# A two-layer encoder on one core: gate and up start together, one fewer output-projection unit, three split buffers, shorter bias and softmax

## The chip, the core and the metric

The kernel runs on one core of a Trainium2 chip. The metric is the device time of one execution in microseconds. The engines are named as in the profile: PE (TensorE matmuls), PEld (its weight loads), ACT (ScalarE), DVE (VectorE), POOL (GpSimd) and SP (SyncE, which issues most DMAs).

## The reference

The inputs are 256 positions of width 1024, in fp32; there are two layers, each an attention sublayer and a feed-forward sublayer, each with a residual.

```python
def mixer_sublayer(x, ...):
    h = rms_norm(x, n1)
    qa, ka, va, qd, kd, vd, qc, kc, vc = split(h @ w_in_l)
    qa, ka = rms_norm(qa, qg[0]), rms_norm(ka, kg[0])
    out_a = neighbourhood_attention(qa, ka, va, rpb_l, ...)      # 4 heads, bias from rpb
    qd, kd = partial_rotary(rms_norm(...)), ...
    out_d = dilated_window_attention(qd, kd, vd, ...)            # 6 heads
    qc, kc = axial_rotary(rms_norm(...)), ...
    out_c = gqa_block_attention(qc, kc, vc)                      # 6 heads, 2 of keys and values
    mix = concatenate([rms_norm(out_a, ..), rms_norm(out_d, ..), rms_norm(out_c, ..)])
    return x + mix @ w_out_l

def channel_sublayer(x, n2, w_gu, cw, cb, w_dn):
    g, u = split(rms_norm(x, n2) @ w_gu)                         # 2 x 2816 wide
    g = depthwise_conv_centred(g, cw, cb)                        # 3 positions
    return x + (gelu(g) * u) @ w_dn
```

Scores are scaled by 1/8. The neighbourhood heads add a relative bias `rpb` and see only keys within a window.

## The kernel before

**Numbers.** Each fp32 product is made of three matmuls on a high and a low part of both factors (`mm3`, L586; in the feed-forward two, with both parts of the input side by side in a 512 wide moving operand). Activations are split when they are turned (`split_T`, L599: PE transposes 128x128 blocks of `const_x` into `psw`, ACT writes the high part, DVE the low part, into `act_hT`). A weight **unit** has at most 2048 columns on 128 partitions: SP loads it into a `wp_raw` buffer (`load`, L538), then in pieces ACT casts it to `wp_hi` and DVE subtracts into `wp_lo` (`split`, L560). `unit` (L575) hands out the next one, and records the load and the split of later ones: `RAWS, PARTS, AHEAD` (L42) are the raw buffers, the split pairs, and how many units the splits run ahead.

**Order of the work.** `Plan` (L217) records every operation. `order` (L289) then schedules them as a list: at each step it takes, of the operations whose inputs, buffers and engine are ready first by a cost model of its own, the one of lowest rank; the rank is the place in the program plus what `later` adds (`SPLIT_LATER`, `TURN_LATER`, `MIX_LATER`, `PREP_LATER`, L53 on). `emit` (L388) issues them in that order; it fixes each engine's queue, SP's too. All instructions so have one line in the profile, L393, and are told apart by the names of their tiles.

**A layer.** The input is normalised and turned, both halves (L732). `projections` (L737) makes, in `psa` banks, dq, dk, dv, cq, ckv, aqk and av, each of one or two units. Beside them the heads run, in pairs: dilated (`d`), grouped (`c`), neighbourhood (`a`). For each group `prep_d`, `prep_c` and `prep_a` (L1030 to L1061) form `rstd` on POOL (`rstd_of`, L591: `small_ms`, `small_rstd`), scale, and rotate by tables that POOL makes from `const_rot` and the gains (`act_cdq`, `act_sdq`, `act_ccq` and so on, L809, L824). `scores` (L1088) multiplies queries and keys into `psw`, `softens` (L942) takes the maximum (`small_mx`), makes its negative (`small_nm`), and ACT forms the exponentials; `turn` transposes `act_s2k` and splits it into `act_ch` and `act_cl`; `weigh` multiplies with the values; `mixed` (L998) writes `act_mixT_hi`, `act_mixT_lo` and the squares `act_sqm`, which POOL adds. `group_rstd` (L1013) sums the squares with a matmul by `ones` and forms the group's `rstd`; the group's output projections (`out_projections`, L761; tiles po in `psa`) follow, and DVE adds them, scaled, to the residual `const_x`. `OUT_ORDER` has three groups, each in two halves of 512 columns, a unit each; the neighbourhood heads' group comes last.

**The neighbourhood bias.** `na_load` (L692) reads the needed rows of `rpb` into `act_few`; `na_repeat` (L706) scales them on POOL, repeats them 64 times into `act_nab` (28 x 1984) and writes these to a scratch buffer in device memory (`dram_scr`); `na_diagonals` (L716) reads them back along diagonals into `act_nab`, so that each query has its row; `na_bias_mask` (L1076) adds the window's mask in three POOL operations of 128x576. For layer 0 this is recorded beside the first projections, for layer 1 at feed-forward steps 2, 3 and 4 of layer 0 (`NA_STEPS`, L1285); `order` is free to issue the parts sooner.

**From attention to the feed-forward.** Recorded in this order: the first half of the last group's projection, the transposes of half 0 of the new residual, the second half of the projection, the mean square, and then gate step 0 (`half_up(first=True)`, L1196): 16 matmuls on input half 0 (k below 4), the transposes of half 1, 16 matmuls on half 1, and `row_scale`, two transposes that spread the row's `rstd`. Up step 0 follows, 32 matmuls in its own `psw` banks.

**The feed-forward.** 11 steps of 256 columns. `gate` (L1241) joins the high and low sums, multiplies by the row scale, convolves (DVE and ACT) and applies Gelu; `up` (L1260) multiplies with it and splits; `down` (L1270) accumulates into four `psa` banks. The order is G0, U0, G1, D0, U1, G2, D1, U2 and on to G10, U10, D9, D10.

Of the kernel before, what the change touches and what calls it, by code (L numbers as in the profile page):

```python
# [41 lines left out]
RAWS, PARTS, AHEAD, CHUNK = 4, 2, 2, 512  # L42
# [174 lines left out]
class Plan:  # L217
    def __init__(self, tc):
        self.tc, self.ops, self.shift, self.burst, self.bursts = tc, [], 0, None, {}
        for name, short in (("tensor", "PE"), ("scalar", "ACT"), ("vector", "DVE"), ("gpsimd", "POOL"), ("sync", "SP")):  # L220
            setattr(self, name, PlanEngine(self, short, getattr(tc.nc, name)))
# [11 lines left out]
    @contextmanager  # L233
    def together(self):

        self.burst = len(self.bursts)
        self.bursts[self.burst] = []
        yield
        self.burst = None

    def add(self, engine, method, args, kw):
# [39 lines left out]
        for v in outs:  # L281
            v.tile.writes.append((i, v.footprint()))
        o.before.discard(i)
# [152 lines left out]
def encoder_kernel(  # L436
# [84 lines left out]
    def units_of(l):  # L521
# [5 lines left out]
        for gi, c0 in OUT_ORDER:  # L527
            yield rows(w_out[l], *OUTP[gi], c0, 512)
# [6 lines left out]
    views = [v for l in range(DEPTH) for v in units_of(l)]  # L535
    raws, parts, taken = [], [], [0]
# [23 lines left out]
    def split(i):  # L560
# [7 lines left out]
        for c in range(0, n, h):  # L568
# [147 lines left out]
    def na_diagonals(l):  # L716
        scr = nabs["scr"]
        for i in range(2):
# [3 lines left out]
            )  # L722

    load(0)
    for l in range(DEPTH):
# [81 lines left out]


        def tables_d(which, g):  # L809
            cd = act.tile([P, NT, HD], F32, tag=f"cd{which}", name=f"cd{which}{l}", bufs=1)  # L810
            sd = act.tile([P, NT, 16], F32, tag=f"sd{which}", name=f"sd{which}{l}", bufs=1)
            b = lambda v: v.unsqueeze(1).to_broadcast([P, NT, v.shape[1]])
            nc.gpsimd.tensor_tensor(cd, rot[:, :, 0:64], b(g[:, l, 1]), op=ALU.mult)
            for i in range(2):
                o, n = (8 * i, 8 * (1 - i)), 8
                nc.gpsimd.tensor_tensor(
                    sd[:, :, o[0] : o[0] + n],
                    rot[:, :, 64 + o[0] : 64 + o[0] + n],
                    b(g[:, l, 1, o[1] : o[1] + n]),
                    op=ALU.mult,  # L820
                )
            return cd, sd

        def tables_c(which, g):  # L824
            cc = act.tile([P, NT, HD], F32, tag=f"cc{which}", name=f"cc{which}{l}", bufs=1)
            sc = act.tile([P, NT, HD], F32, tag=f"sc{which}", name=f"sc{which}{l}", bufs=1)
            b = lambda v: v.unsqueeze(1).to_broadcast([P, NT, v.shape[1]])
            nc.gpsimd.tensor_tensor(cc, rot[:, :, 80:144], b(g[:, l, 2]), op=ALU.mult)
            for i in range(4):
                o, n = (16 * i, 16 * (i ^ 1)), 16  # L830
                nc.gpsimd.tensor_tensor(
                    sc[:, :, o[0] : o[0] + n],
                    rot[:, :, 144 + o[0] : 144 + o[0] + n],
                    b(g[:, l, 2, o[1] : o[1] + n]),
                    op=ALU.mult,
                )
            return cc, sc
# [99 lines left out]
        class Head:  # L937
# [4 lines left out]
            def softens(self, sps):  # L942
# [4 lines left out]
                mx = small.tile([P, NT], F32, tag="mx", name=f"mx_{name}")  # L947
                rs = small.tile([P, NT], F32, tag="rs", name=f"rs_{name}")
                if bias is not None:
                    sb = act.tile([P, NT, S], F32, tag="s2k", name=f"sb_{name}", bufs=NS2K)  # L950
                    for t in range(NT):
                        nc.vector.tensor_tensor_reduce(
                            sb[:, t], sps[t], bias[t], SCALE, -3e38, ALU.add, ALU.max, mx[:, t : t + 1]
                        )
                    nc.vector.tensor_scalar_mul(nm, mx, -1.0)
                    for t in range(NT):
                        nc.scalar.activation(
                            p[:, t], sb[:, t], AF.Exp, bias=nm[:, t : t + 1], accum_out=rs[:, t : t + 1]
                        )
                else:  # L960
                    for t in range(NT):
                        nc.vector.reduce_max(mx[:, t : t + 1], sps[t], axis=AX.X)
                    nc.vector.tensor_scalar_mul(nm, mx, -SCALE)
                    for t in range(NT):
                        nc.scalar.activation(
                            p[:, t], sps[t], AF.Exp, bias=nm[:, t : t + 1], scale=SCALE,
                            accum_out=rs[:, t : t + 1],
# [62 lines left out]
        def prep_d(which, g):  # L1030
            cd, sd = tables_d(which, g)
# [9 lines left out]
        def prep_c(which, g):  # L1041
            cc, sc = tables_c(which, g)
# [33 lines left out]
        def na_bias_mask():  # L1076
            for i in range(1, NR, 9):
                nv = nabs[l][:, i : i + 9]
                nc.gpsimd.tensor_tensor(
                    nv, nv, na_mask.unsqueeze(1).to_broadcast([P, 9, GRID_W]), op=ALU.add  # L1080
# [115 lines left out]
        def half_up(name, first=False):  # L1196

            wh, wl = unit()
            ps = [psw.tile([P, 2, S], F32, tag="w", name=f"{name}{j}") for j in range(2)]

            def part(j, k):
                js = slice(j * P, (j + 1) * P)
# [3 lines left out]
            if first:  # L1206
                for k in range(4):
                    part(0, k)
                for k in range(4):
                    part(1, k)  # L1210
                split_T(halves(1), h2_hi, h2_lo, 4, gains[:, 2, l, 4:8], f"n2{l}1")
                for k in range(4, KD):
                    part(0, k)
# [163 lines left out]
```

## Time and profile before

| | us |
|---|---|
| median of 3 runs | 625.4 |
| lowest and highest | 625.36, 627.85 |
| the profiled execution, its own time | 626.01 |
| its span in the trace | 624.2 |
| granted clock, mean | 1.00 |
| PE, PEld busy | 608.7, 525.0 |
| DVE, ACT, POOL busy | 490.3, 430.6, 83.3 |
| steady feed-forward, layers 0 and 1 | 148 to 315, 438 to 620 |

The span runs from the first to the last instruction of the trace; the execution's own time is a little longer. Times in the views are from the span's start. A timeline row gives start, duration, engine, line, operation, output and inputs, shapes, and the number of instructions put together in the row; in brackets stands how long the engine was idle before it, and whose end it waited for. Buffer numbers are left out of names.

### The profile page before, as it was taken

How to read it: one execution, taken by the hardware profiler on the slowest of the kernel's cores; microseconds unless marked ns; L12 is line 12 of the kernel's file. 1: busy time of each engine (PE TensorE's matmuls, PEld its weight loads, DVE VectorE, ACT ScalarE, POOL GpSimd, SP SyncE). 2: the span in 40 equal slices, each digit the busy share in tenths (PEclk: the TensorE clock that was granted, in tenths of full speed). 3: DMA queues.
4: the chain of work that ended last, by engine and by line, in shares of the span. 5: the costliest groups of instructions: out<-in, count | busy, mean ns of one | idle time of the engine just before them, and what ended most of it. 6: DMA issues, size and time to landing. Idle time of an engine off the chain costs nothing.

```text
span 624.2 us, 9846 instructions
## 1 busy us (share of the span) xinstructions
PE 608.7 (98%) x3496; PEld 525.0 (84%) x3496; DVE 490.3 (79%) x1026; ACT 430.6 (69%) x1064; POOL 83.3 (13%) x131
## 2 busy tenths in 40 slices
PE   8999999989999999999999999998999999999997
PEld 6998888778888888888899979786888888888885
DVE  4889889798777777777867798978877777877775
ACT  6887998677655655565588799888765655566552
POOL 2764231340000000000023210312000000000000
PEclk9999999999999999999999999999999999999999
DMA  8794312866555555555444632043565655555511
GB/s 279 262 287 154 102 40 96 249 154 213 189 177 178 199 202 202 179 172 173 153 145 154 225 102 85 34 138 136 202 207 199 202 188 170 187 199 188 170 49 67
DMA packets 81345, 104.66 MB, mean 168 GB/s; under 512 B 9464, under 2 KB 68952, under 8 KB 81296
## 3 DMA queue, kind: packets, MB, share of 16 engines
q1 hardware_dynamic: 80720, 103.51, 51.0%
q8 instruction: 27, 0.44, 0.3%
q10 hardware_dynamic: 576, 0.53, 0.3%
q14 instruction: 22, 0.18, 0.1%
HBM read 102.54 MB, written 1.49 MB: 167 GB/s over the span
## 4 chain that ended last, share of the span: by engine, by line
PE 86%; ACT 4%; DVE 4%; DMA 3%; POOL 1%; issue 1%; SPq 0%; ACTq 0%; POOLq 0%; DVEq 0%
PE psw_w L393 47%; PE psa_a L393 39%; ACT act_s2k L393 2%; DMA act_nab<-dram_scr 1%; DVE wp_lo L393 1%; DMA dram_scr<-act_nab 1%; DVE act_s2k L393 1%; POOL small_rstd L393 1%; DVE act_hT L393 1%; DMA act_s2k<-in_norm_g_dram 1%; POOL act_nab L393 0%; ACT L393 0%; ACT wp_hi L393 0%; DVE const_x L393 0%; DVE act_z L393 0%
## 5 line engine op out<-in xcount | busy, mean ns | idle before, releaser
L393 DVE TENSOR_TENSOR wp_lo<-wp_raw,wp_hi 128x512 fp32r<-128x512 f32 (+2 forms) x348 | 248.3, 742 | 50.9 <-ACT wp_hi L393 49.1
L393 PE MATMUL psw_w<-act_hT,wp_hi 128*128 128x512 f32 x704 | 247.4, 396 | 4.7 <-DVE act_hT L393 4.7
L393 ACT CAST wp_hi<-wp_raw 128x512 fp32r<-128x512 f32 (+2 forms) x348 | 213.7, 658 | 25.1 <-PE psw_w L393 15.6
L393 PE MATMUL psw_w<-act_hT,wp_lo 128*128 128x256 f32 x704 | 195.7, 279 | 0.0
L393 PEld LDWEIGHTS psw_w<-act_hT,wp_hi 128*128 128x128 f32 x704 | 131.8, 188 | 36.8 <-DVE act_hT L393 5.9
L393 PEld LDWEIGHTS psw_w<-act_hT,wp_lo 128*128 128x128 f32 x704 | 132.6, 188 | 1.1
L393 PE MATMUL psa_a<-wp_hi,act_hT 128*128 128x384 f32 (+2 forms) x448 | 114.9, 335 | 0.0
L393 ACT COPY act_s2k<-psw_w 128x256 f32<-128x256 f32 x88 | 32.3, 372 | 81.1 <-PE psw_w L393 81.1
L393 PEld LDWEIGHTS psa_a<-wp_hi,act_hT 128*128 128x128 f32 x448 | 78.6, 190 | 2.3
L393 PE MATMUL psa_a<-wp_lo,act_hT 128*128 128x384 f32 (+2 forms) x224 | 74.6, 334 | 0.0
L393 PE MATMUL psa_a<-wp_lo,act_ch 128*128 128x512 f32 x176 | 69.5, 395 | 0.0
L393 PE MATMUL psa_a<-wp_hi,act_ch 128*128 128x512 f32 x176 | 69.4, 394 | 0.0
L393 PE MATMUL psa_a<-wp_hi,act_cl 128*128 128x512 f32 x176 | 66.2, 395 | 0.2 <-DVE act_cl L393 0.2
L393 DVE TENSOR_TENSOR act_s2k<-psw_w,act_s2k 128x256 f32<-128x256 f32 x88 | 36.8, 422 | 30.6 <-ACT act_s2k L393 30.0
L393 PEld LDWEIGHTS psa_a<-wp_lo,act_hT 128*128 128x128 f32 x224 | 42.5, 190 | 2.1 <-DVE wp_lo L393 1.0
L393 PEld LDWEIGHTS psa_a<-wp_hi,act_cl 128*128 128x128 f32 x176 | 33.2, 188 | 8.3 <-DVE act_cl L393 0.6
L393 PEld LDWEIGHTS psa_a<-wp_hi,act_ch 128*128 128x128 f32 x176 | 33.1, 188 | 7.7
L393 PEld LDWEIGHTS psa_a<-wp_lo,act_ch 128*128 128x128 f32 x176 | 33.1, 188 | 6.9
L393 DVE SCALAR_TENSOR_TENSOR act_s2k<-act_s2k,act_cw,act_s2k 128x255 f32<-128x255 f32 x88 | 36.7, 476 | 1.4 <-ACT act_s2k L393 1.3
L393 ACT ACTIVATE act_s2k<-act_s2k,act_cw 128x256 f32<-128x256 f32 x44 | 24.1, 595 | 13.3 <-DVE act_s2k L393 13.3
L393 POOL TENSOR_TENSOR small_rstd<-small_ms,const_mh 128x6 f32<-128x6 f32 (+2 forms) x26 | 31.3, 1203 | 2.1
L393 ACT ACTIVATE act_s2k<-act_s2k,small_rs 128x256 f32<-128x256 f32 x64 | 28.8, 506 | 3.3 <-DVE small_rs L393 3.3
(110 smaller groups left out, 764.0 us busy)
## 6 DMA issues: line engine op xcount, KB each, us to landing
wp_raw<-in_w_gate_up_dram SPq DMA_DIRECT2D x44, 1024.0 KB, 5.0
wp_raw<-in_w_down_dram SPq DMA_DIRECT2D x22, 1024.0 KB, 4.8
wp_raw<-in_w_in_dram SPq DMA_DIRECT2D x14, 768.0 KB, 4.8
wp_raw<-in_w_in_dram SPq DMA_DIRECT2D x8, 1024.0 KB, 5.5
wp_raw<-in_w_out_dram SPq DMA_DIRECT2D x8, 768.0 KB
wp_raw<-in_w_out_dram SPq DMA_DIRECT2D x4, 512.0 KB, 3.7
act_nab<-dram_scr SPq DMA_DIRECT2D x4, 448.0 KB, 6.7
out_dram<-const_x SPq DMA_DIRECT2D x4, 256.0 KB, 2.0
```

Of the source, the lines that this page charges most:

```text
L393: getattr(o.engine.real, o.method)(*map(real, o.args), **{k: real(v) for k, v in o.kw.items()})
```

## The change

- `RAWS, PARTS, AHEAD` go from 4, 2, 2 to 3, 3, 3: three raw buffers, three split pairs, splits up to three units ahead.
- `first_halves` replaces the first gate step: gate on half 0, the transposes of half 1, up on half 0 (in two `psa` banks), gate on half 1, the row scale, up on half 1.
- The last group of the output projection is one unit of 2 x 1024 columns, one DMA per layer in place of two; its pieces are split so that the first 512 columns of both rows come first.
- `softens`: the maximum is made negative in the same instruction (a minimum with `-SCALE`, or `negate`), the `small_nm` step goes, and ACT's scale is -1 or 1. For the grouped heads the factor 1/8 moves into the query gains, one more POOL operation per layer.
- The bias: the scaling of `act_few` on POOL goes; the mask is added by DVE, which scales in the same instruction.
- The tables of layer 1 are made at feed-forward step 4 of layer 0. `not_before(engine)` makes what is recorded within it come, in the planner's order, after all that was recorded for that engine so far; it is used for the parts of layer 1's bias (SP) and for these tables (POOL). It holds the order only, and adds no wait to the program.

The numbers of PE and ACT instructions are the same in both programs; SP issues 2 fewer, DVE 26 fewer, POOL 6 fewer. The resulting orders differ in more places than the diff names. In layer 0 of the changed program the copy into `act_nab` stands ahead of the first `rstd` of the dilated queries on POOL. The write to `dram_scr` is SP's 18th entry, ahead of the load of raw unit 7; the reads back are ahead of raw unit 8. DVE's first mask add is ahead of the low part of the turned dilated keys (`act_ko`), after the splits of unit cq; the second is ahead of the first dilated softmax. In layer 0, 11 matmuls of the last output-projection group stand behind the matmuls with `ones`, where there were 21; DVE takes two split pieces of up step 0 before the last steps of `const_x`, and in layer 1 the same before the very last one.

```diff
-RAWS, PARTS, AHEAD, CHUNK = 4, 2, 2, 512
+RAWS, PARTS, AHEAD, CHUNK = 3, 3, 3, 512
...
+    def not_before(self, engine):
+
+        self.behind = max(i for i, o in enumerate(self.ops) if o.engine.name == engine)
+        yield
+        self.behind = None
...
+        if self.behind is not None:
+            o.before.add(self.behind)
...
-            yield rows(w_out[l], *OUTP[gi], c0, 512)
+            if gi < 2:
+                yield rows(w_out[l], *OUTP[gi], c0, 512)
+            elif c0 == 0:
+                yield rows(w_out[l], *OUTP[gi], 0, D)
...
-        for c in range(0, n, h):
+        starts = range(0, n, h)
+        if i % PER_LAYER == LAST_OUT:
+
+            h = CHUNK
+            starts = [k * b + c for c in range(0, b, h) for k in range(a)]
+        for c in starts:
...
-        nc.gpsimd.tensor_scalar(nabs["few"], nabs["few"], ISCALE, None, ALU.mult)
...
+    def tables_c(l, which):
+        g = gains_of[which][:, l, 2]
+        if which == "q":
+            nc.gpsimd.tensor_scalar(g, g, SCALE, None, ALU.mult)
...
-                wh, wl = unit()
+                if gi < 2:
+                    wh, wl = unit()
+                else:
+                    if h == 0:
+                        hold["out"] = unit()
+                    wh, wl = (z[:, :, h : h + 512] for z in hold["out"])
...
-                            sb[:, t], sps[t], bias[t], SCALE, -3e38, ALU.add, ALU.max, mx[:, t : t + 1]
+                            sb[:, t], sps[t], bias[t], -SCALE, 3e38, ALU.add, ALU.min, nm[:, t : t + 1]
                         )
-                    nc.vector.tensor_scalar_mul(nm, mx, -1.0)
...
-                        nc.vector.reduce_max(mx[:, t : t + 1], sps[t], axis=AX.X)
-                    nc.vector.tensor_scalar_mul(nm, mx, -SCALE)
+                        nc.vector.reduce_max(nm[:, t : t + 1], sps[t], axis=AX.X, negate=True)
...
-                nc.gpsimd.tensor_tensor(
-                    nv, nv, na_mask.unsqueeze(1).to_broadcast([P, 9, GRID_W]), op=ALU.add
+                nc.vector.scalar_tensor_tensor(
+                    nv, nv, ISCALE, na_mask.unsqueeze(1).to_broadcast([P, 9, GRID_W]), ALU.mult, ALU.add
                 )
...
+        def first_halves():
+
+            G, U = banks(psw, "w", f"G{l}_0"), banks(psa, "a", f"U{l}_0")
+            ws = unit()
+            for j in range(2):
+                products(G, ws, j, range(4))
+            split_T(halves(1), h2_hi, h2_lo, 4, gains[:, 2, l, 4:8], f"n2{l}1")
+            wu = unit()
+            for j in range(2):
+                products(U, wu, j, range(4))
+            for j in range(2):
+                products(G, ws, j, range(4, KD))
+            row_scale()
+            for j in range(2):
+                products(U, wu, j, range(4, KD))
+            return G, U
...
             if kind == "G" and l + 1 < DEPTH and s in NA_STEPS:
-                NA_STEPS[s](l + 1)
+                with nc.not_before("SP"):
+                    NA_STEPS[s](l + 1)
+            if kind == "G" and l + 1 < DEPTH and s == 4:
+                with nc.not_before("POOL"):
+                    tables_of(l + 1)
```

`products(ps, ws, j, ks)` is the inner loop of the former `half_up` over the given k.

More of the change, by code (lines that the diff above doesn't have):

```diff
@@ L806, in encoder_kernel @@
             gk = gk.rearrange("p (l a d) -> p l a d", l=DEPTH, d=HD)
[L809 to L815, printed above, removed]
-                nc.gpsimd.tensor_tensor(
[L817 to L837, printed above, removed]
+            gains_of.update(q=gq, k=gk, rot=rot)
         def normed(ps, nh, t, name):
@@ L1030, in prep_d @@
         def prep_d(which, g):
-            cd, sd = tables_d(which, g)
+            if ("d" + which, l) not in tables:
+                tables["d" + which, l] = tables_d(l, which)
+            cd, sd = tables["d" + which, l]
             for t in range(NT):
@@ L1041, in prep_c @@
         def prep_c(which, g):
-            cc, sc = tables_c(which, g)
+            if ("c" + which, l) not in tables:
+                tables["c" + which, l] = tables_c(l, which)
+            cc, sc = tables["c" + which, l]
             nh = H_GQ if which == "q" else H_GKV
@@ L1242, in gate @@
             nm = f"{l}_{s}"
-            Gs = joined(half_up(f"G{nm}", s == 0), f"Gs{nm}")
+            if s == 0:
+                hold["G"], hold["U"] = first_halves()
+            Gs = joined(hold["G"] if s == 0 else half_up(f"G{nm}"), f"Gs{nm}")
             nc.vector.tensor_tensor(Gs, Gs, rb.unsqueeze(1).to_broadcast([P, 2, S]), op=ALU.mult)
@@ L1261, in up @@
             nm = f"{l}_{s}"
-            C = joined(half_up(f"U{nm}"), f"C{nm}")
+            C = joined(hold["U"] if s == 0 else half_up(f"U{nm}"), f"C{nm}")
             nc.vector.tensor_tensor(C, made[s], C, op=ALU.mult)
```

74 lines of the change are left out of this document (49 added, 25 removed).

## Prediction

> **What bounds the kernel now.** I read the page's busy shares first, then the waits of PE, then a table of stages, then the timelines around the places where PE stands still.
>
> ```profile
> span 624.2 us, 9846 instructions
> ## 1 busy us (share of the span) xinstructions
> PE 608.7 (98%) x3496; PEld 525.0 (84%) x3496; DVE 490.3 (79%) x1026; ACT 430.6 (69%) x1064; POOL 83.3 (13%) x131
> ```
>
> PE (TensorE matmul) is busy for 608.7 of 624.2 us. The change removes no matmul: both programs issue the same number. So it can win only from the 624.2 - 608.7 = 15.5 us in which PE is idle, and it can lose by adding to them. The waits of PE (columns: total us, times, longest us) name who ends that idle time:
>
> ```profile
> PE psw_w L393 <- DVE act_hT L393: 4.7, 4, 1.9
> PE psw_w L393 <- ACT act_s2k L393: 2.7, 4, 1.1
> ...
> PE psw_w L393 <- ACT act_ch L393: 0.6, 2, 0.3
> PE psw_w L393 <- DVE act_cl L393: 0.5, 1, 0.5
> PE psa_a L393 <- DVE const_x L393: 0.4, 1, 0.4
> PE psw_w L393 <- POOL act_sqm L393: 0.3, 1, 0.3
> ```
>
> The largest, 4.7 us in four waits, is the first feed-forward step waiting for `act_hT`, the normalised and turned input that DVE writes. Two waits lie in each layer, one per half of the input. The table by stage (window; its length; busy us and instructions of PE, PEld, DVE, ACT, POOL; clock; DMA share; GB/s) shows where there is room:
>
> ```profile
> 116.00:127.00 11.00, 9.35 (x49) 6.88 (x48) 9.38 (x18) 6.55 (x17) 1.63 (x3) 1.00 1.01 243
> 127.00:148.00 21.00, 19.06 (x110) 16.28 (x110) 19.79 (x33) 15.93 (x34) 7.01 (x6) 1.00 0.49 156
> 148.00:315.50 167.50, 167.30 (x871) 141.91 (x871) 126.69 (x214) 99.59 (x183) 0.00 (x0) 1.00 0.56 187
> ...
> 620.00:624.20 4.20, 0.48 (x3) 0.04 (x1) 0.75 (x1) 0.00 (x0) 0.00 (x0) 0.98 0.35 130
> ```
>
> From 148 to 315.5 us, the steady feed-forward of layer 0, PE is idle for 0.2 us: nothing is to be had there. The last 3.7 idle us are the output's way out, which the change doesn't touch. What is left is the stretch where attention ends and the feed-forward begins (116 to 148: 1.65 + 1.94 us idle), its twin in layer 1, and single waits in the projections. The granted clock is 1.00 in all these stages.
>
> **The change, part by part.**
>
> **Gate and up begin together.** These are the PE rows of the first step (start, duration, what it writes and reads, count, and in brackets the idle time before it):
>
> ```profile
> 126.89 0.50 PE L393 MATMUL psw_w<-act_hT,wp_hi 128*128 128x512 f32 x1 [0.18 <-DVE act_hT L393]
> ...
> 129.78 1.04 PE L393 MATMUL psw_w<-const_ident,const_x 128*128 128x128 f32 x8
> ...
> 132.75 0.50 PE L393 MATMUL psw_w<-act_hT,wp_hi 128*128 128x512 f32 x1 [1.94 <-DVE act_hT L393]
> ...
> 438.58 0.50 PE L393 MATMUL psw_w<-act_hT,wp_hi 128*128 128x512 f32 x1 [1.01 <-DVE act_hT L393]
> ```
>
> The gate's first 16 matmuls take 129.78 - 126.89 = 2.9 us, eight transposes follow, and then PE waits 1.94 us (1.01 in layer 1) for the second half of `act_hT`. In the changed order 16 matmuls of up, also on the first half, stand in that gap: 2.9 us of work that PE would do later anyhow. 2.9 is more than 1.94 and than 1.01, so both waits should go: **-1.94 - 1.01 = -2.95 us**. The up unit must be split by then; three split buffers allow it. The two waits ahead of the first half (0.18, and 4.7 - 0.18 - 1.94 - 1.01 = 1.6 in layer 1) stay, since nothing on the first half can start before it. Behind the second half nothing new is late: the row scale now lies between gate's and up's second 16.
>
> The price is on DVE. In layer 1 the changed order puts two split pieces of up ahead of the last step of `const_x`, on which the first transposes and so the first half depend. A piece is worth about 0.6 us (the rows below: four in 3.73 us with POOL beside them, one 128x512 pass of the residual 0.74). That delay is between 0 and 1.2 us; I take half, **+0.6**, as DVE has some idle time there to absorb it.
>
> **The mask leaves POOL.** Three views: POOL's timeline, the PE row that pays, DVE's timeline.
>
> ```profile
> 25.43 2.19 POOL L393 COPY act_nab<-act_few 28x1984 f32<-28x1984 f32 x1
> ...
> 38.23 0.39 POOL L393 TENSOR_TENSOR act_sdk<-const_rot,const_gk 128x16 f32<-128x16 f32 x2
> 44.65 2.81 POOL L393 TENSOR_TENSOR act_nab<-act_nab,const_na 128x576 f32<-128x576 f32 x2 [6.03 <-DMA act_nab<-dram_scr]
> 47.56 0.60 POOL L393 TENSOR_SCALAR small_ms<-small_ss,small_he 128x6 f32<-128x6 f32 x1
> 48.24 1.34 POOL L393 TENSOR_TENSOR small_rstd<-small_ms,const_mh 128x6 f32<-128x6 f32 x1
> ```
> ```profile
> 53.84 0.33 PE L393 MATMUL psw_w<-const_ident,act_s2k 128*128 128x128 f32 x1 [1.12 <-ACT act_s2k L393]
> ```
> ```profile
> 38.43 1.08 DVE L393 TENSOR_TENSOR wp_lo<-wp_raw,wp_hi 128x384 fp32r<-128x384 f32 x2
> 39.50 1.02 DVE L393 TENSOR_TENSOR act_ko<-psw_w,act_ko 128x384 fp32r<-128x384 f32 x2
> ...
> 46.07 1.95 DVE L393 TENSOR_TENSOR wp_lo<-wp_raw,wp_hi 128x512 fp32r<-128x512 f32 x1 [1.27 <-ACT wp_hi L393]
> ...
> 127.92 0.74 DVE L393 SCALAR_TENSOR_TENSOR const_x<-psa_a,small_rstd,const_x 128x512 f32<-128x512 f32 x1
> 128.58 3.73 DVE L393 TENSOR_TENSOR wp_lo<-wp_raw,wp_hi 128x512 fp32r<-128x512 f32 x4
> ```
>
> POOL stands 6.03 us behind the bias's DMA, then adds the mask for 2.81 us, and only then forms the `rstd` of the GQA queries at 48.24. DVE, with that and its softmax work queued in order, is late, and PE waits 1.12 us at 53.84. In the changed program POOL no longer touches the mask, so the wait of 6.03 and the 2.81 leave that chain; **-1.12 us** (between 0, if something else is late at 53.84, and 1.12). The three adds per layer go to DVE: by 128 x 512 in 0.74 us, a pass of 128x576 is 0.83 us; the upper end is POOL's own 2.81 / 2 = 1.4. Six of them are 5.0 to 8.4 us of DVE, against this row of the groups (busy us, mean ns, idle before):
>
> ```profile
> L393 DVE TENSOR_SCALAR small_nm<-small_mx 128x2 f32<-128x2 f32 x32 | 6.5, 203 | 0.0
> ```
>
> The 32 negations that the shorter softmax drops are 6.5 us of DVE, so DVE's load stays about where it was. Neither is on PE's path by itself: each negation saves a head's chain 0.2 us, and other heads' matmuls cover it. I cost both at **0**; without that cover they would be worth at most -0.2 for each of the last heads, and +0.8 for a mask add.
>
> **Transfer order for layer 0's bias.** The write to the scratch buffer and the reads back stand earlier in SP's queue.
>
> ```profile
> 30.10 0.52 SPq L393 DMA_DIRECT2D dram_scr<-act_nab  x1
> ...
> 35.48 1.73 SPq L393 DMA_DIRECT2D act_nab<-dram_scr  x2
> ```
>
> From the write's issue to the mask's start are 44.65 - 30.10 = 14.6 us. I estimate the new issue at about 23, as soon as the copy (25.43 in before, now ahead of the first `rstd`) is done; the landing is then near 37.5. DVE reaches the first mask, between the rows 38.43 and 39.50, at about that time: no wait, **0**. The copy's 2.19 us now stand ahead of the first dilated `rstd`; PE has projections queued, so this too is 0, at worst +2.2.
>
> **Three raw and three split buffers, one output-projection unit instead of two halves.** Together the buffers hold six units, as before, and the bytes are the same. No PE wait in the list is for a weight transfer. Splits run one unit further ahead, which lets PE fill the waits at the end of attention (0.6 + 0.5 + 0.4 + 0.3 = 1.8 at most in the list) with output-projection matmuls. But in layer 0 only 11 of those, where there were 21, are then left behind the sum of squares, and the chain from there to the first `act_hT` is as long as it was: what is filled ahead opens behind. Bounds -1.8 to +2.3 (10 matmuls of about 0.23 us); I take **0**.
>
> **Tables and the second bias in the feed-forward.** 14 POOL operations, the copy and the bias's DMAs for layer 1 move to steps 2 to 4, where POOL is idle (0.00 of 167.5) and DMA at 0.56. **0**; rival D has the price.
>
> The sum: -2.95 + 0.6 - 1.12 = -3.5 us. The profiled execution took 626.0 us (span 624.2), 0.6 over the median 625.4; on the median the forecast is **621.9 us**.
>
> **The rivals.**
>
> **A, what is saved goes again.** The end of attention is one chain (softmax, turn, weigh, squares, `rstd`, residual, transposes, `act_hT`). If DVE, at 9.38 of 11.00 us before 127, reaches the first half later because up's split pieces stand ahead of it, the wait of 0.18 grows to about what the second half gave. For: DVE is the busiest engine beside PE there. Against: POOL's masks at 128.94 to 136 no longer slow its splits (3.73 us for four, where four times 0.62 would be 2.5). Only the 1.1 at 53.84 is left: 624.3.
>
> **B, more goes.** All four `act_hT` waits (4.7), the 1.12 and most of the 1.8: 7.3 us, so 618.1. For: DVE loses its collisions with POOL and has slack. Against: the first half's chain has no new cover.
>
> **C, slower: DVE waits for the bias.** The mask is now an instruction of DVE, in its queue ahead of `act_ko`, and a DMA feeds it. Behind it stand `act_ko`, then every split. PE needs `act_ko` for the scores at about 46.2, so a landing up to some 44 costs nothing. If the reads land no earlier than before (44.65), the price is about 1. If the earlier issue meets the projections' weights and the 14.6 us from write to mask become 28, from 23 to 51, DVE stands still for 12 us and PE for 7: 625.4 - 3.5 + 7 = 628.9. It ends slower than before from a landing of about 48. For: 6.03 us is what POOL waited for the same transfer. Against: the issue is some 7 us earlier.
>
> **D, POOL beside the splits.** At 46.07 a split piece beside POOL's mask took 1.95 us, and at 128.58 four took 3.73. The copy (2.19) and the tables (two in 0.39 by the row 38.23, so fourteen in 2.8, the wider ones longer: some 4 us) now run beside the steady feed-forward. If each us of POOL takes one from DVE, the steps 3 and 4 lose 2 and 4 us of it. DVE has 167.5 - 126.69 = 40.8 idle over ten steps, 4.1 a step, which would just cover it; a burst that makes one split late could cost PE half of the tables' time, 2 us: 625.4 - 3.5 + 2 = 623.9. Against: at 38.23 such tables ran, and DVE's two pieces from 38.43 took 0.54 each.
> [...]
>
> **E, it does not do what it says**: up's split isn't done in time, PE stands at up's first half instead, and the time is that of before, 625.4.
>
> **How the numbers follow.** About 0.5%, 3.1 us, is what a measurement of this kernel can tell from no change, so faster is below 622.3. The forecast (620.2 to 623.5) has 0.40, of which 0.25 lies below 622.3; A 0.16, B 0.17, C 0.17, D 0.05, E 0.05. Faster: 0.25 + 0.17 = 0.42. Same: 0.15 + 0.16 + 0.05 + 0.05 = 0.41. Slower: 0.17. The range goes from 617.0 (B with 1 us more) to 627.5 (into C), which leaves out some 0.04 below and 0.11 above.
>
> **What would show it.** Right: PE's waits for `act_hT` fall from four to two and from 4.7 to about 2.3 us; the wait before the first softmax's turn at 54 is gone; no mask on POOL; DVE's mask adds last about 0.83 us with no idle time for a DMA before them; the steady steps stay at 0.2 us idle. Wrong: a longer wait for the first half (A), a DVE idle for `act_nab` near 39 us (C), PE idle between 190 and 230 us (D), or a wait for `wp_lo` at up's first half (E).

## The result, and the profile after

| | before | after |
|---|---|---|
| median, runs on one chip, us | 625.73 (4 runs, 625.36 to 627.85) | 620.3 (4 runs, 620.02 to 621.88) |
| ratio, with 95% interval | | 0.9912 (0.9883 to 0.994) |
| profiled execution's span, us | 624.2 | 618.7 |

The kernel became faster by 5.4 us; 3.5 to 3.8 were forecast (621.9), and 620.3 lies in the range of 617.0 to 627.5, at the lower edge of what the forecast itself covered (620.2 to 623.5).

Where it came from is read with landmarks: the starts of the same matmuls in both PE timelines, and the differences of neighbours. Single traces differ here too: among the traces of this section and the next, four have the changed kernel's order of PE, DVE and ACT up to layer 0's first gate matmul (the changed kernel itself, a_nofirst, a_tables and a_warm), and layer 0's attention takes 80.8, 81.0, 81.7 and 81.6 us in them. Layer 1's takes 79.08 to 79.13. So a difference of under 1 us in layer 0's attention says little.

| stage, us | before | after | change |
|---|---|---|---|
| start to layer 0's first scores | 46.17 | 46.45 | +0.28 |
| layer 0, first scores to first gate matmul | 80.72 | 80.81 | +0.09 |
| first gate matmul to layer 1's first projection | 190.06 | 187.36 | -2.70 |
| layer 1, first projection to first scores | 35.25 | 34.93 | -0.32 |
| layer 1, first scores to first gate matmul | 81.42 | 79.13 | -2.29 |
| first gate matmul to the last matmul | 186.46 | 185.75 | -0.71 |
| last matmul to the end of the span | 4.12 | 4.27 | +0.15 |

Two changes I had forecast are there, the starts of the feed-forwards (-2.70, -0.71). One I had forecast is missing: layer 0's attention should have gained 1.12 and gained nothing. One I had not forecast is there: layer 1's attention (-2.29, where I had +0.6).

The page of the changed kernel, and PE's waits (total, times, longest, us):

```profile
span 618.7 us, 9836 instructions
## 1 busy us (share of the span) xinstructions
PE 606.9 (98%) x3496; PEld 526.2 (85%) x3496; DVE 487.8 (79%) x1000; ACT 427.0 (69%) x1064; POOL 79.9 (13%) x125
```
```profile
PE psw_w L402 <- DVE act_hT L402: 2.7, 2, 1.4
PE psw_w L402 <- ACT act_s2k L402: 2.0, 3, 1.2
```

The waits for `act_hT` fell from four to two and from 4.7 to 2.7 us, as forecast (two, about 2.3); but layer 0's is 1.43, where 0.18 was to stay, and layer 1's 1.24, where some 2.2 was expected. PE's idle time fell from 15.5 to 618.7 - 606.9 = 11.8 us, by 3.7. The other 1.8 of the span's 5.5 us is PE's busy time, 608.7 before, with the same number of matmuls: the prediction's first step, that the change can win only from idle time, does not hold. What made the busy time shorter is not settled. These are the rows in layer 0 in which PE stands still in the changed kernel, in order of time:

```profile
51.98 0.33 PE L402 MATMUL psw_w<-const_ident,act_s2k 128*128 128x128 f32 x1 [0.29 <-ACT act_s2k L402]
...
84.93 0.66 PE L402 MATMUL psw_w<-const_ident,act_s2k 128*128 128x128 f32 x4 [1.16 <-ACT act_s2k L402]
...
124.29 0.44 PE L402 MATMUL psw_w<-const_ident,const_x 128*128 128x128 f32 x2 [0.43 <-DVE const_x L402]
124.95 0.88 PE L402 MATMUL psw_w<-const_ident,const_x 128*128 128x128 f32 x6 [0.22 <-DVE const_x L402]
127.25 0.50 PE L402 MATMUL psw_w<-act_hT,wp_hi 128*128 128x512 f32 x1 [1.43 <-DVE act_hT L402]
```

The wait of 1.12 at 54 is 0.29 at 52 in this trace, but that is chance: in a_nofirst, a_twoout, a_tables and a_warm, which have the same order of PE's matmuls up to there, it is 0.52, 1.18, 1.19 and 1.08. New waits stand at 84.93 (1.16, where none was) and at the first half of `act_hT` (1.43, where there were 0.18). What layer 0's attention saved was spent again inside it: the outcome of rival A, in this one place, though by other mechanisms than A's (a_twoout and a_mix below). The steady feed-forward is untouched, tables and all:

```profile
150.00:310.00 160.00, 160.00 (x835) 135.89 (x834) 127.47 (x211) 94.59 (x174) 13.30 (x18) 1.00 0.61 192
```

PE is busy for 160.00 of 160.00 us, with POOL at work for 13.30 of them. Rival D is out.

### The profile page after: what moved, and what is told of

The parts are those of the page before. It is cut to its first block, busy times and chain, and to the rows that moved or that the text cites. A ratio compares the mean times of both kernels' runs of the same rounds, so it can differ in the third digit from the quotient of the medians.

```text
span 618.7 us, 9836 instructions
## 1 busy us (share of the span) xinstructions
PE 606.9 (98%) x3496; PEld 526.2 (85%) x3496; DVE 487.8 (79%) x1000; ACT 427.0 (69%) x1064; POOL 79.9 (13%) x125
## 4 chain that ended last, share of the span: by engine, by line
PE 89%; ACT 4%; DMA 3%; DVE 3%; issue 1%; POOL 0%; ACTq 0%; DVEq 0%
PE psw_w L402 49%; PE psa_a L402 40%; DMA wp_raw<-in_w_in_dram 2%; ACT act_s2k L402 2%; DVE wp_lo L402 1%; ACT wp_hi L402 1%; DMA act_s2k<-in_norm_g_dram 1%; DVE const_x L402 0%; ACT act_z L402 0%; DVE small_nm L402 0%; DVE act_z L402 0%; POOL small_rstd L402 0%; DVE act_qo L402 0%; ACT act_ch L402 0%; DVE act_hT L402 0%
## 5 line engine op out<-in xcount | busy, mean ns | idle before, releaser
L402 PE MATMUL psw_w<-act_hT,wp_hi 128*128 128x512 f32 x672 | 236.3, 396 | 2.7 <-DVE act_hT L402 2.7
L402 PE MATMUL psw_w<-act_hT,wp_lo 128*128 128x256 f32 x672 | 187.3, 279 | 0.0
L402 PEld LDWEIGHTS psw_w<-act_hT,wp_hi 128*128 128x128 f32 x672 | 126.0, 188 | 33.4 <-DVE act_hT L402 3.3
L402 PEld LDWEIGHTS psw_w<-act_hT,wp_lo 128*128 128x128 f32 x672 | 126.6, 188 | 0.9
L402 ACT COPY act_s2k<-psw_w 128x256 f32<-128x256 f32 x84 | 30.9, 373 | 82.0 <-PE psw_w L402 81.9
L402 PE MATMUL psa_a<-wp_hi,act_cl 128*128 128x512 f32 x176 | 69.0, 395 | 0.0
L402 DVE TENSOR_TENSOR act_s2k<-psw_w,act_s2k 128x256 f32<-128x256 f32 x84 | 35.4, 423 | 36.2 <-ACT act_s2k L402 35.2
L402 PE MATMUL psw_w<-act_ch,const_v 128*128 128x256 f32 x128 | 28.5, 286 | 0.6 <-ACT act_s2k L402 0.6
```

Source lines behind the costliest of these rows:

```text
L402: getattr(o.engine.real, o.method)(*map(real, o.args), **{k: real(v) for k, v in o.kw.items()})
```

## The experiments

The kernels run on one chip share runs of the kernel before; each ratio is to those. Single runs differ by some us with PE's granted clock, of which more at the end (the runs of a_nofirst with a mean of at least 0.999 take 622.84 to 623.76 us, those at 0.993 to 0.997 take 624.38 to 626.24); the column "full clock" has the median of the runs with a mean granted clock of at least 0.999 and how many they are. Before has 625.4, 625.9 and 625.3 in that column in the three groups, the changed kernel 620.1 (3 of 4); so some tenths between kernels of different groups, or on two or three runs, say nothing.

| run | median us | ratio to before, 95% | full clock |
|---|---|---|---|
| a_nofirst | 624.07 | 0.9962 (0.9945 to 0.9979) | 623.5 (6 of 12) |
| a_422 | 625.03 | 0.9983 (0.9964 to 1.0001) | none of 12 |
| a_twoout | 617.27 | 0.9845 (0.9819 to 0.9871) | 617.3 (4 of 4) |
| b_333_first | 625.6 | 0.9974 (0.9953 to 0.9996) | 622.9 (2 of 12) |
| a_negs | 623.6 | 0.9943 (0.9922 to 0.9964) | 622.2 (2 of 5) |
| a_poolmask | 623.57 | 0.9947 (0.9925 to 0.997) | 621.4 (3 of 10) |
| a_late | 627.66 | 1.0015 (0.9997 to 1.0034) | none of 10 |
| a_tables | 620.33 | 0.9897 (0.9873 to 0.9921) | 619.7 (2 of 4) |
| a_warm | 620.25 | 0.9898 (0.9881 to 0.9915) | 620.2 (5 of 6) |
| a_twoout_mix | 615.33 | 0.9832 (0.981 to 0.9853) | 615.3 (4 of 5) |
| a_mix | 616.47 | 0.9843 (0.9821 to 0.9866) | 615.4 (3 of 4) |
| b_333 | 629.25 | 1.0062 (1.0039 to 1.0086) | 627.7 (4 of 12) |

The name begins with the kernel that was edited: a for the changed one, b for the one before. In a_negs, a_poolmask, a_late and a_warm the planner's order was kept and only the named instructions exchanged or moved; in the others the planner made a new order.

**a_nofirst: gate's first step alone, up after it.**

```diff
-            G, U = banks(psw, "w", f"G{l}_0"), banks(psa, "a", f"U{l}_0")
+            G = banks(psw, "w", f"G{l}_0")
...
-            wu = unit()
-            for j in range(2):
-                products(U, wu, j, range(4))
...
-            for j in range(2):
-                products(U, wu, j, range(4, KD))
```

> The changed kernel with gate's first step as before the change: up starts after gate is done, in its own psw banks; nothing else. Up to layer 0's first gate matmul the order is that of the changed kernel. Theory: up's 16 matmuls covered the wait for the second half of act_hT, so the stage from the first gate matmul to the next layer's first projection grows from 187.4 to about 190.1 us, that of layer 1 from 185.7 to about 186.5: 623.7 us, the waits for act_hT four again with 1.9 and 1.0 among them. Rival: the first half's chain sets the pace anyway and the wait is refilled: under 1 us, 621.

At full clock 623.5 against 620.1: 3.4 us back, and 623.7 was expected. The waits for `act_hT` are four again:

```profile
PE psw_w L402 <- DVE act_hT L402: 4.7, 4, 1.4
```

The first theory holds; what up covered doesn't return as another wait. The waits for the second half are 1.01 us in each layer (rows at 133.72 and 437.46), where 1.9 and 1.0 were expected: 0.9 of layer 0's 1.94 had gone by other parts of the change. The two waits are 2.0 of the 3.4 us; where the rest lies the trace doesn't show cleanly, as the profiled execution has a mean granted clock of 0.993.

**a_422: four raw and two split buffers.**

```diff
-RAWS, PARTS, AHEAD, CHUNK = 3, 3, 3, 512
+RAWS, PARTS, AHEAD, CHUNK = 4, 2, 2, 512
```

> The changed kernel with four raw and two split buffers, two units ahead, as before the change. Theory: layer 1's attention lost 2.6 us (116.7 to 114.1 from its first projection to its first gate matmul) because splits three units ahead leave PE an output-projection matmul for each wait; with two it goes back to about 116.7, and the first up half may wait for its split: 623 us or more. Rival: the shorter softmax and the mask on DVE brought it, and the buffers do nothing: 620.3.

It became slower, but not where I said. First scores to first gate matmul take 78.18 and 77.32 us, shorter than with three split buffers (80.81 and 79.13). The loss is behind the first gate matmul, where a split comes late (rows of PE):

```profile
144.50 0.73 PE L402 MATMUL psw_w<-act_hT,wp_hi 128*128 128x512 f32 x2 [1.56 <-ACT wp_hi L402]
147.12 0.39 PE L402 MATMUL psw_w<-act_hT,wp_lo 128*128 128x256 f32 x1 [1.88 <-DVE wp_lo L402]
...
450.02 0.73 PE L402 MATMUL psw_w<-act_hT,wp_hi 128*128 128x512 f32 x2 [1.55 <-ACT wp_hi L402]
451.33 0.39 PE L402 MATMUL psw_w<-act_hT,wp_lo 128*128 128x256 f32 x1 [0.58 <-DVE wp_lo L402]
```

So the theory that splits further ahead shortened layer 1's attention falls, and its rival "the buffers do nothing" too: three split buffers lengthen attention in the changed kernel, and are needed where gate and up hold two units at once.

**a_twoout: the last group in two units again.**

```diff
-            if gi < 2:
-                yield rows(w_out[l], *OUTP[gi], c0, 512)
-            elif c0 == 0:
-                yield rows(w_out[l], *OUTP[gi], 0, D)
+            yield rows(w_out[l], *OUTP[gi], c0, 512)
```

> The changed kernel with the last output-projection group in two units of 512 columns, as before the change. Theory: same bytes, same pieces, no wait for a transfer: within 0.5 us of 620.3. Rival: one unit less is what puts the splits of gate and up ahead in time, and layer 1's end of attention gets its 2.3 us back: 622.6.

Neither: it is 2.9 us faster than the changed kernel, 2.1 to 2.5 of them at layer 0's first gate matmul (124.97, against 127.25 in the changed kernel and 127.06 and 127.46 in a_tables and a_nofirst). The matmuls by `ones`, with which the chain to `act_hT` begins, first in the changed kernel and then in this one:

```profile
120.62 0.50 PE L402 MATMUL psw_w<-const_ones,act_sqm 128*128 128x1 f32 x4
```
```profile
117.98 0.50 PE L402 MATMUL psw_w<-const_ones,act_sqm 128*128 128x1 f32 x4
```

With the one unit split early, the planner leaves 11 of its matmuls behind `ones`, with two units 22. The 11 ahead delay the chain by 2.6 us, and are missing behind it, where PE then waits 0.43, 0.22 and 1.43. With two units the trace shows no wait at these three places.

**b_333_first and b_333: the kernel before, with the buffers and the first halves, and with the buffers alone.**

```diff
-RAWS, PARTS, AHEAD, CHUNK = 4, 2, 2, 512
+RAWS, PARTS, AHEAD, CHUNK = 3, 3, 3, 512
```

b_333_first has `first_halves` as well, as in the change.

> The kernel before with two parts of the change alone: three raw, three split buffers, and gate's and up's first halves together. Masks, softmax, tables and the two last units stay as before. Theory: the feed-forward starts give 3.4 us and layer 1's attention 2.6: about 619.7. Rival: layer 1's attention owes its gain to the softmax and the mask, so only 3.4: 622.3.

> The kernel before with three raw and three split buffers alone. If the buffers by themselves are worth nothing in attention (81.1 against 81.4 in layer 1 with the first halves beside them), stages and time stay within 0.5 us of 625.4 at the full clock. Rival: early splits crowd DVE here too: 1 to 2 us slower in each attention, 628.

At full clock 627.7 with the buffers alone (2.4 slower than before) and 622.9 with the first halves too (2.5 faster than before): together the first halves are worth 4.8 here. First gate matmul to next projection is 190.11 and 187.69, in layer 1 187.25 and 185.32. Layer 1's attention stays at 81.1 in both, against 81.4 before, so its gain in the changed kernel comes from neither. The total of b_333 is that of its rival (628), but not its reason: with the kernel before's order early splits cost nothing in layer 1's attention.

**a_negs: the 32 negations back, in the changed kernel's order.**

```diff
-    sb[:, t], sps[t], bias[t], -SCALE, 3e38, ALU.add, ALU.min, nm[:, t : t + 1]
+    sb[:, t], sps[t], bias[t], SCALE, -3e38, ALU.add, ALU.max, nm[:, t : t + 1]
...
+    nc.vector.tensor_scalar_mul(nm, nm, -1.0)      # behind the second maximum
```

> The changed kernel in exactly its order, with the 32 negations back as instructions of DVE (128x2, in place, behind each head's second maximum; the two exponentials follow it). Both kernels with three split buffers and with two had layer 1's attention short (first scores to first gate matmul 79.1 and 77.3 us against 81.4 before), and the kernel before with only the buffers and the first halves had 81.1. So the theory now is that the softmax steps made it: 79.1 goes to about 81, layer 0 gains the like, 623 to 624 us. Rival: other heads' matmuls cover each 0.2 us, as I had costed it: within 0.5 us of the changed kernel.

First scores to first gate matmul: 82.58 and 80.61 us, that is 0.9 to 1.8 more in layer 0 than the four traces without the negations, and 1.5 more in layer 1; 2.1 us at full clock. The wait of PE at 52 is 1.78, where those traces have 0.29 to 1.19:

```profile
52.67 0.33 PE L418 MATMUL psw_w<-const_ident,act_s2k 128*128 128x128 f32 x1 [1.78 <-ACT act_s2k L418]
```

The theory holds for 1.5 of layer 1's 2.29 us.

**a_poolmask: the mask back on POOL, in the changed kernel's order.**

```diff
-    nc.vector.scalar_tensor_tensor(nv, nv, ISCALE, mask, ALU.mult, ALU.add)
+    nc.gpsimd.tensor_tensor(nv, nv, mask, op=ALU.add)     # and few scaled on POOL
```

> The changed kernel in exactly its order, with the six mask additions (and the scaling of the 28x31 rows) back on POOL. If POOL beside DVE is what made the wait of 1.12 us at 54: split pieces of 1.9 us beside the masks again, the wait there back to about 1, and in layer 1, where the masks lie beside the steady feed-forward, nothing: 621 us. Rival, as I had predicted it: the chain of POOL (mask, then rstd) made it, and since the reads now land before POOL needs its next rstd, nothing comes back: 620.3.

1.3 us slower at full clock, and all of it in layer 0 (first gate matmul at 128.71, against 127.06 to 127.46; first scores to first gate matmul 82.66, against 80.81 to 81.7; layer 1 79.11 against 79.13). POOL, DVE and PE around it, a row of each view and two of PE:

```profile
52.81 1.47 POOL L407 TENSOR_TENSOR act_nab<-act_nab,const_na 128x576 f32<-128x576 f32 x1
```
```profile
52.93 1.76 DVE L407 TENSOR_TENSOR act_z<-act_z,act_sw 128x384 f32<-128x384 f32 x1
```
```profile
52.20 0.33 PE L407 MATMUL psw_w<-const_ident,act_s2k 128*128 128x128 f32 x1 [0.91 <-ACT act_s2k L407]
...
54.74 0.55 PE L407 MATMUL psw_w<-const_ident,act_z 128*128 128x128 f32 x3 [1.18 <-DVE act_z L407]
```

A DVE step that takes 0.55 in the changed kernel takes 1.76 beside POOL's mask, and PE waits 1.18 for it. POOL's first `rstd` comes no later for the mask here (48.15 against 48.35), since POOL was idle ahead of it; the second, behind a mask, starts 0.4 later and is done 1.8 before DVE takes it. What costs is this DVE step beside the mask, and not POOL's chain.

**a_late: the reads of layer 0's bias as late as the order allows.**

```diff
+    done = [i for i in done if i not in reads]
+    at = done.index(masks[0])
+    done[at:at] = reads
```

> The changed kernel with one thing moved: SP issues the two reads of layer 0's bias as the last thing before the first mask, behind the weight loads that stood between, everything else in its order. Rival C of the prediction: DVE then waits for the landing with the low part of the keys and the splits behind it; issued near 38 to 44, it lands near 46 to 52, PE stands still for what exceeds 44, 2 to 8 us: 622 to 628. If DVE has more slack than I gave it: under 1 us, 621.

DVE and PE of this kernel, and the windows around (start and end; length; busy us of PE and the others; granted clock as the third number from the end):

```profile
49.14 0.76 DVE L413 SCALAR_TENSOR_TENSOR act_nab<-act_nab,const_na 128x576 f32<-128x576 f32 x1 [9.11 <-DMA act_nab<-dram_scr]
```
```profile
50.42 1.90 PE L413 MATMUL psw_w<-act_ko,act_qo 64*128 64x256 f32 x11 [3.41 <-DVE act_ko L413]
```
```profile
48.00:50.00 2.00, 0.00 (x0) 0.00 (x0) 0.86 (x2) 0.00 (x0) 0.00 (x0) 0.69 0.72 261
50.00:52.00 2.00, 1.58 (x11) 1.40 (x11) 2.00 (x5) 0.52 (x1) 0.00 (x0) 0.50 0.03 12
52.00:54.00 2.00, 2.00 (x12) 1.78 (x11) 2.00 (x5) 1.14 (x11) 0.00 (x0) 0.50 0.00 0
```

Rival C is a real mechanism: with the landing at 49.1 DVE stands still for 9.11 us, PE for 3.41, and the granted clock falls to 0.69 over the window from 48 and 0.50 over the two behind it. The kernel loses all it had gained. I had put PE's loss at 5 for such a landing; the wait alone is 3.4, so the point from which it costs is nearer 46 than 44.

**a_tables: layer 1's tables made in layer 1.**

```diff
-                with nc.not_before("POOL"):
-                    tables_of(l + 1)
```

> The changed kernel with layer 1's rotation tables made where they are needed, in layer 1, as before the change. Theory: POOL has time there; first scores to first gate matmul of layer 1 stays at 79.1, within 0.5 us of the changed kernel, and the steady feed-forward loses nothing either way. Rival: POOL's 14 operations beside DVE's softmax are part of layer 1's 2.3 us: 622.

620.33 us, and 79.12 us in layer 1's attention: no difference.

**a_mix and a_twoout_mix: splits two units ahead in attention, three for the feed-forward's start.** a_twoout_mix also has the two units of a_twoout.

```diff
+            ahead = AHEAD if i % PER_LAYER >= PER_LAYER - len(FFN) - 2 else 2
-            while len(parts) < min(i + AHEAD, len(views)):
+            while len(parts) < min(i + ahead, len(views)):
```

> The changed kernel, one output-projection unit, with splits two units ahead until two units before gate's first and three from there on. Theory of the early splits: 616 to 618 us. Rival: no change from 620.3 or slower.

> The changed kernel with two output-projection units as in the run without the one unit (617.3), and splits only two units ahead until two units before gate's first, three from there on; loads three ahead throughout. With two buffers first scores to first gate matmul took 78.2 and 77.3 us against 80.8 and 79.1. Theory: early splits crowd DVE and ACT beside the softmax; two ahead there and three for up's first half gives both gains: 614 to 616 us. Rival: the fourth raw buffer did it, or the order by chance: 617 or more.

616.47 and 615.33: both beat both kernels, the second by 5.0 us on the changed one and by 1.7% on the one before. First scores to first gate matmul in layer 1 take 77.42 and 77.17 us, as with two split buffers, while the feed-forwards keep their gain (187.20 and 187.20 us behind the first gate matmul, 185.29 and 185.31 in layer 1). The theory was that early splits crowd DVE and ACT beside the softmax. The times agree with it, but the rows show another reason at the wait of 84.93. PE turns the exponentials of one pair of heads at 84.93 in the changed kernel, after 1.16 us of waiting, and at 84.55 in a_mix, without a wait:

```profile
84.55 0.60 PE L402 MATMUL psw_w<-const_ident,act_s2k 128*128 128x128 f32 x4
```

From the start of the scores ahead of it to there it is 3.04 us in the one and 3.21 in the other, so the softmax is no faster. But a_mix has 16 projection matmuls (`psa_a<-wp_hi,act_hT` and `wp_lo`) between 82.55 and 84.55, where the changed kernel has none left: with its splits further ahead it had started the last one at 81.68. What runs ahead is missing as cover, as with the one unit. Whether the same accounts for layer 1's 1.7 us is open.

In a_twoout_mix the longest wait for `act_hT` is halved:

```profile
PE psw_w L402 <- DVE act_hT L402: 1.3, 2, 0.7
```

**a_warm: PE's stop ahead of the first gate matmul filled.**

```diff
+    nc.tensor.matmul(flat, warm, moving, start=True, stop=True)     # ten times, overwritten
```

> The changed kernel in exactly its order, with ten matmuls of ones (128x256, bf16; their result is overwritten) ahead of the first gate matmul of each layer, where PE stands still for 1.4 and 1.2 us. Seen so far: wherever a trace has a granted clock under 1, it lies right behind such a stop of PE, at 0.50 for about 4 us. Theory: the stop sets it off; with the stop filled for most of its length no run has a mean clock under 0.998, the median is that of the undisturbed runs of the changed kernel, 620 us. Rival: the dip comes from the chip whatever PE does; about as many runs have it as of the changed kernel's relatives, half or more, and the median is 621 to 624.

```profile
126.83 1.25 PE L407 MATMUL psw_w<-const_warm 128*128 128x256 bf16 x10
128.43 0.50 PE L407 MATMUL psw_w<-act_hT,wp_hi 128*128 128x512 f32 x1 [0.34 <-DVE act_hT L407]
```

Five of six runs have the full clock; the sixth, with a mean of 0.997, is the profiled one. Its low stretch is not here: from 128.43 on the matmuls take their usual time (at 129.48 one of 128x512 is followed by the next at 129.71, 0.23 us later, as in the changed kernel at 128.29 and 128.52).

## Why the prediction was right, and where it was not

- **Up in the gap (-2.95).** Right in mechanism and nearly in size: -2.70 and -0.71, and 3.4 us when it is undone. That the sum of the waits, 2.95, is so near is in part luck: with the rest of the change the two waits would have been 2.0. It is the part on which the forecast stands.
- **Up's split pieces ahead of the residual (+0.6 in layer 1).** Wrong: no delay is seen. The wait for the first half in layer 1 became 1.24 where it had been 1.59, first before and then after:

```profile
433.62 0.50 PE L393 MATMUL psw_w<-act_hT,wp_hi 128*128 128x512 f32 x1 [1.59 <-DVE act_hT L393]
```
```profile
428.67 0.50 PE L402 MATMUL psw_w<-act_hT,wp_hi 128*128 128x512 f32 x1 [1.24 <-DVE act_hT L402]
```

- **The mask off POOL (-1.12).** The wait did not go (0.29 to 1.19 in traces of the same order), and my step to it was wrong. I let POOL's mask hold up the `rstd` at 48.24. After the change that `rstd` starts at 48.35, no earlier, since POOL there waits for ACT's squares:

```profile
47.83 0.44 POOL L402 TENSOR_SCALAR small_ms<-small_ss,small_he 128x6 f32<-128x6 f32 x1 [10.52 <-ACT act_s2k L402]
48.35 1.35 POOL L402 TENSOR_TENSOR small_rstd<-small_ms,const_mh 128x6 f32<-128x6 f32 x1
```

  In before POOL's wait of 6.03 had hidden that the squares would have come at about the same time. What cost PE 1.12 was a DVE step made slower by the mask beside it. The prediction read only the two masks ahead of the `rstd`; the third stands beside the chain on which PE waits. POOL, DVE and ACT before:

```profile
51.33 1.42 POOL L393 TENSOR_TENSOR act_nab<-act_nab,const_na 128x576 f32<-128x576 f32 x1
```
```profile
51.45 1.72 DVE L393 TENSOR_TENSOR act_z<-act_z,act_ccq 128x384 f32<-128x384 f32 x1
53.10 0.15 DVE L393 RECIPROCAL small_rs<-small_rs 128x2 f32<-128x2 f32 x1
```
```profile
53.28 0.91 ACT L393 ACTIVATE act_s2k<-act_s2k,small_rs 128x256 f32<-128x256 f32 x2 [2.48 <-DVE small_rs L393]
```

  The same DVE step takes 0.55 in the changed kernel, 1.17 less, and the reciprocal behind it is what ACT and then PE waited for. In the changed kernel the first turn comes 5.5 to 6.4 us after the first scores, where it came after 7.7. PE waits all the same, since the planner's new order has 34 projection matmuls in between, where it had 45. Putting the masks back on POOL in that order costs 1.3 us (a_poolmask). I had that mechanism, but only in rival D, where it was harmless. Beside the mask the two DVE steps of 128x384 take 1.72 and 1.76 us, and 0.55 each without it; why, no run shows. The masks on DVE take 0.74 each (0.83 estimated), without a wait for the DMA:

```profile
40.14 0.74 DVE L402 SCALAR_TENSOR_TENSOR act_nab<-act_nab,const_na 128x576 f32<-128x576 f32 x1
```

- **The negations (0).** The step that failed by most. I said other heads' matmuls cover each head's 0.2 us; a_negs puts 0.9 to 1.8 us on layer 0's attention and 1.5 on layer 1's, 2.1 in all at full clock. The cover isn't complete: the planner's order leaves a head's chain through DVE and ACT as what PE waits for in several places.
- **The one unit (0, between -1.8 and +2.3).** The bound was right, the value taken wrong: it costs 2.1 to 2.5 us in layer 0, by the very mechanism named for the upper end. The matmuls that move ahead of `ones` open behind it.
- **The buffers (0).** Alone they cost 2.4 us. The prediction weighed how many units are held, and not that splits which come sooner let PE spend its projection matmuls sooner; a_mix, which splits later in attention only, gets back 4.7 at full clock. That DVE and ACT are crowded beside the softmax stays a theory, and of b_333's own 2.4 no row is known.
- **The tables, and the bias's transfers (0).** Right.
- The sum was near because the errors cancelled: too little for the softmax, too little against the buffers and the one unit. By the runs at full clock, undone or done alone: first halves -3.4, negations -2.1, mask -1.3, one unit +2.9, buffers +2.4, together -1.5 against -5.3 measured. The rest isn't settled. An edit that makes the planner order anew moves more than itself, so these prices don't add; those in the kept order (negations, mask) are the firm ones.

## What to carry to other kernels

Work that is already split and independent, put into the gap between two halves of a dependency, is worth the gap (a_nofirst: two waits of 1.01 us come back, and 3.4 us in all); but what is moved ahead of the start of a chain both delays the chain and is missing behind it (the changed kernel beside a_twoout: 2.6 us of delay, and waits of 0.43, 0.22 and 1.43). A small step taken off each head's chain counts when the busy engine waits for such chains, however full that engine is (a_negs: 32 steps of 0.2 us are 2.1 us, with PE busy for 98% of the changed kernel's span). Loads and splits that run further ahead are not free (a_mix: 4.7 us less with the splits later in attention): the matmuls that they release are done sooner and are missing as cover later, as at 84.93, where PE waits 1.16, so the depth should follow the stage.

## What the runs showed of the hardware

After a short stop of PE the granted clock can be 0.50 for some us. The profiled executions of all experiments but a_twoout have a mean granted clock of 0.988 to 0.997, a_twoout's has 1.000. In windows of 2 us a low stretch begins in or directly behind a stop of PE: in b_333 and b_333_first behind one of 1.01 us (0.98, 0.50 and 0.67 from 118 on; 0.54 and 0.61 from 120 on), in a_422 behind two of 1.56 and 1.88 (0.99, 0.50 and 0.65 from 146 on) and two of 1.55 and 0.58 (0.94, 0.50 and 0.71 from 450 on). Behind the last of these a matmul of 128x512 starts 0.43 us after the one ahead of it (452.23 and 452.65), and 0.24 once the clock is back (455.66 and 455.90). Each of the four stretches, summed over its windows, is 1.7 us of full clock lost, so by this estimate 3.4 us at 0.50. In a_late, with a stop of 3.41, it is about twice that: from within the window at 48 (0.69) to the rows of PE at 55.4 (from 54.76 three matmuls of 128x256 take 0.64 us, from 55.84 three take 0.36). In a_tables PE stood still for 1.4 us, after two waits of 0.6 us together:

```profile
126.00:128.00 2.00, 0.94 (x3) 0.84 (x4) 2.00 (x6) 2.00 (x7) 0.00 (x0) 0.81 0.51 176
128.00:130.00 2.00, 2.00 (x7) 1.61 (x7) 1.51 (x4) 1.67 (x5) 1.53 (x3) 0.50 0.00 0
130.00:132.00 2.00, 2.00 (x14) 1.82 (x13) 0.56 (x1) 0.00 (x0) 0.00 (x0) 0.83 0.10 18
```

0.81, 0.50 and 0.83 over 2 us each are again 1.7 us of full clock lost. PE started 7 matmuls in the second window and 14 in the third. The same stop (1.43) is in the changed kernel's own trace, and the clock there is 1.00 from 124 to 132, so the dip follows it in some executions and not in others. Of the runs of before shared by the first four kernels 14 of 29 had the full clock, of a_twoout, with no stop at that place in layer 0 (it has three of 1.1 to 1.2 us elsewhere), 4 of 4, of a_422 (stops of up to 1.88 us) none of 12 and of a_late (3.41) none of 10. The stop costs its own length and, at times, some 1.7 us more: full-clock runs of a_nofirst have a median of 623.5, the others lie between 624.38 and 626.24. That filling the stop prevents the dip is not shown by a_warm's six runs: five had the full clock, against 11 of 20 of the kernels with the stop (the changed one, a_nofirst, a_tables).

What sets the clock to 0.50, and what ends it, no run here shows.
